# Sliding-window attention trunk on one core: scores by 32 queries and 160 keys, and a written order for the attention stage

## The chip, the cores and the metric

The kernel runs on one core of a Trainium2 chip. The metric is the device time of one execution in microseconds (us). The profile is one execution taken by the hardware profiler; its times are counted from the first instruction. Engines: PE is the matrix engine (PEld its weight loads), DVE the vector engine, ACT the scalar engine, POOL GpSimd, SP the engine that issues most DMAs. L389 is line 389 of the kernel before.

## The reference

One layer of a trunk on 512 tokens of width 2048, all in float32. Conv, state-space and forgetting attention do not occur, since the depth is 1 and mixer 0 is the sliding-window attention:

```python
hn = rmsnorm(x, norm_g)
q, k, v, gate = split(hn @ w_in)              # 32 heads of 64, 4 key/value heads of 64
scores = einsum('qd,jd->qj', q, k) * 64**-0.5 + bias[query - key]   # per head
scores = where(0 <= query - key < 128, scores, min)
m = maximum(scores.max(), sink)
e = exp(scores - m)
probs = e / (e.sum() + exp(sink - m))
y = ((probs @ v) * silu(gate)) @ w_out
x = x + y
g = sigmoid(rmsnorm(x, ple_norm) @ ple_gate)
x = x + (p @ ple_proj) * g
return rmsnorm(x, final_g)
```

## The kernel before

Every product is done in three matmuls of a narrower float32 form: each operand is split into a high part (a cast) and a low part (the rest), and `mm3` (L120 to L122) adds high by high, low by high and high by low. So each weight tile of 128 by 1024 costs one cast on ACT (`whi`, L106; later `bhi`, L575) and one subtraction on DVE (`wlo`, L107; `blo`, L576).

The stages, in order of the program:

1. First steps (L185 to L256): 16 chunks of the model width. Each loads a piece of x and of the first weights, splits both, and PE adds it into the sums of keys (`ktps`), values (`vps`) and the first two query pairs (`qps`). For chunk 0 the weights come in two DMAs, and their first 256 columns are split by DVE alone (L200, L201). `xl` (L202) is the low part of x.
2. Seam (L271 to L305): the sums leave PSUM. Queries go to `q` as high and low halves (`evac_q`), keys are scaled by `rb` (1/rms of every token) and split (`make_key`), values likewise (`split`).
3. Attention and projections, about 84 to 457 us. An outer loop runs over 64 blocks plus 3: block i has d = i // 8, which names four heads (two pairs), and g = i % 8, which names 64 queries. In one pass of the loop PE gets, in this order: two transposes of the probabilities of block i-2 (`turn`, L431), two or three matmuls by the values for block i-3 (`weigh`, L467 and L469), two matmuls of scores for block i (`scores`, L389; one for each pair of heads), and then 7 of the 464 chunk steps of the query and gate projections that are left after the first (`projections`, a step is three matmuls of 512 columns). There are 30 projections, 14 of query pairs and 16 of gates, with 16 steps and two weight tiles each.
4. Output projection, then the gated embedding, both as seven-product block schemes (`ORDER_OUT`, `ORDER_PLE`), and at last four blocks with the norm and the stores. `split_last` (L578 to L586) splits the eight weight tiles of the last product ahead of time, at the places that the table `early` (L954) names: a key (5, 0, 3) means product 5, half 0, after its quarter 3.

In a block of stage 3 the work after the scores is: DVE adds the bias to the high part and then the low part (L398), which also multiplies by `sclq`, the query's 1/rms over 8; a maximum folds the two window ends (L413); a reduction gives the row maximum (L415); ACT takes two exponentials with their sums (L418); DVE a reciprocal (L419); ACT scales the probabilities (L421). After PE's transposes ACT casts to `r` (L433), DVE takes the rest (L434), POOL cuts out the own part (L443, from g = 2 on) and ACT copies half of it (L450); `weigh` reads `r` and `own`. Every second block ACT copies half of the sums to `tmp` (L476) and DVE adds them into `u` (L477). A finished gate projection costs DVE, ACT and DVE one operation each (`open_gate`, L499 to L501), and later one on DVE (`gate_value`, L491).

What sets the order: PE and SP follow the written order throughout (`manual_schedule`). In stage 3 POOL does too; DVE and ACT are ordered by a scheduler that runs when the kernel is built. In the seam and in the last part of stage 4 DVE and ACT are in written order as well. Weight tile n is asked for at the place in the program where it is split (`_make`, L101); the splits are made two tiles ahead of their use (`ahead=2`), with three buffers each for raw, high and low tiles. Since SP waits only for free buffers, it may run ahead of the other engines. Between two passes of the loop, `sum_weights` puts weight additions by DMA on SP and POOL.

The key and value sums, in stage 3, share PSUM with the scores (one buffer of two banks, tag `w`), the transposes (`t`, two), the value sums (`o`, two) and the projections (`p`, two): the sum of projection m takes the bank of m-2.

Of the kernel before, what the change touches and what calls it, by code (L numbers as in the profile page):

```python
# [19 lines left out]
S = 512  # L20
P = 128
# [9 lines left out]
UNITS = S // HB  # L31
BUCKETS = 32
# [7 lines left out]
PAD = 32  # L40
# [13 lines left out]
def trunk_kernel(ctx: ExitStack, tc: tile.TileContext, a: dict):  # L54
# [32 lines left out]
    class Weights:  # L87
# [4 lines left out]

        def add(self, src):
            self.srcs.append(src)
# [6 lines left out]
        def _make(self, i):  # L101
            self.load(i + 1)
# [22 lines left out]
    sinkb = const.tile([P, PAIRS], F32, name="sinkb")  # L125
# [17 lines left out]
    sclq = const.tile([P, UNITS], F32, name="sclq")  # L143
# [24 lines left out]
    q_at = {int(0.5 + 3.516 * (c // 2)) - 2 + c % 2: c for c in range(2, PAIRS)}  # L168
# [15 lines left out]

    for k in range(KC):  # L185
        both = start_pool.tile([P, 2, 768], F32R, tag="w0s", name=f"w0s{k}")
# [50 lines left out]
        if k == 9:  # L237
            run(rsqrt_mean(rstd1, ssq1, D, "r1"))
            for e in range(2):
                for b in range(2):  # L240
                    nc.vector.tensor_scalar_mul(
                        sclq[HB * e : HB * e + HB].rearrange("p (n b) -> p n b", b=2)[:, :, b],
                        rstd1[HB * b : HB * b + HB], HD ** -0.5,
                    )

            rdram = tc.dram_tile([NB, P], F32, name="rdram")
            nc.gpsimd.dma_start(rdram.rearrange("t p -> p t"), rstd1)
            nc.gpsimd.dma_start(rb, rdram.rearrange("t p -> (t p)").partition_broadcast(P))
        if k == 10:
            for e in range(2):  # L250
                nc.sync.dma_start(sinkb[HB * e : HB * e + HB], a["sinks"][e].partition_broadcast(HB))
# [6 lines left out]
    def evac_q(c, ps):  # L258

        q = Q[c] = kvq.tile([P, UNITS, 2, HB], F32R, tag="q", name=f"q{c}", bufs=4)  # L260
        halves = slice(0, 64), slice(64, 128)
        for e in range(2):
            src = ps[halves[e]].rearrange("p (g q) -> p g q", q=HB)
            hi, lo = q[halves[e], :, e], q[halves[1 - e], :, e]
            nc.scalar.copy(hi, src)
            nc.vector.tensor_sub(lo, src, hi.bitcast(F32))


    seam = ExitStack()
    seam.enter_context(  # L270
        tc.manual_schedule(engines={getattr(mybir.EngineType, v) for v in ("PE", "SP", "DVE", "Activation")})  # L271
    )
    for c in range(2):
        evac_q(c, q_ps[c])
# [4 lines left out]
    def make_key(h):  # L279
# [4 lines left out]
        for o in (slice(0, 64), slice(64, 128)):  # L284
            nc.scalar.copy(k[o, 0], kt[t][same])
        for o in (slice(0, 64), slice(64, 128)):
            nc.vector.tensor_sub(k[o, 1], kt[t][same], k[same, 0].bitcast(F32))
# [4 lines left out]
    def split(dst, v):  # L292
        nc.scalar.copy(dst[:, :, 0, :], heads(v))
        nc.vector.tensor_sub(dst[:, :, 1, :], heads(v), dst[:, :, 0, :].bitcast(F32))

    nc.vector.tensor_mul(kt[0], kt_ps[0], rb)
    make_key(0)
# [8 lines left out]
    split(V[0], values[0])  # L306
    seam.close()
# [29 lines left out]
    DV = apool.tile([P, NB - 1, 2, KVH * 2 * HD], F32R, name="DV")  # L337
    diffs = {}

    def make_diff(n):  # L340
# [8 lines left out]
        split(dst.rearrange("p (h l d) -> p h l d", h=KVH, l=2), v)  # L349
# [7 lines left out]
    def first_chores(i):  # L357
        if i == 0:
            for n in range(1, NB):
                make_diff(n)  # L360
        if 1 <= i < NB:
            split(V[i], values[i])
            spread_diff(i)

    def load_bias(d):
        biases[d] = apool.tile([P, 2, P + HB], F32, tag="bias", name=f"bias{d}", bufs=2)
        for e in range(2):
            src = bass.AP(
                tensor=tdram.tensor, offset=tdram.offset + (4 * d + e) * TOEP + HB,
                ap=[[1, HB], [2 * TOEP, 2], [1, P + HB]],  # L370
            )
            nc.sync.dma_start(biases[d][HB * e : HB * e + HB], src)

    def scores(i):

        d, g = divmod(i, UNITS)
        odd = g % 2
# [4 lines left out]
        first = max(g - 2, 0) * HB  # L384
        n = P if g < 2 else P + HB
        s_ps = spsum.tile([P, 2, S], F32, tag="w", name=f"s{i}")
        for u in range(2):
            st = Q[2 * d + u][:, g].rearrange("p e q -> p (e q)")
            nc.tensor.matmul(s_ps[:, u, : 2 * n], st, key[:, :, first : first + n], start=True, stop=True)  # L389
        t = apool.tile([P, 2, 4 + P + HB], F32, tag="t", name=f"t{i}", bufs=4)  # L390
        seen = t[:, :, 65:194] if odd else t[:, :, 0:129]
        pr = t[:, :, 65:193] if odd else t[:, :, 1:129]
        sink = 193 if odd else 0
        nc.gpsimd.tensor_copy(t[:, :, sink], sinkb[:, 2 * d : 2 * d + 2])
        bias = biases[d][:, :, ::-1]

        def add(out, in0, in1):
            nc.vector.scalar_tensor_tensor(  # L398
                out=out, in0=in0, scalar=sclq[:, g : g + 1], in1=in1, op0=ALU.mult, op1=ALU.add
            )  # L400

        if g < 2:
            if g == 0:
                nc.gpsimd.memset(t[:, :, 65:129], MASKED)
            n = HB * (g + 1)
            out = pr[:, :, :n]
            add(out, s_ps[:, :, :n], bias[:, :, 192 - n :])
# [753 lines left out]
```

## Time and profile before

| what | value |
|---|---|
| time, median of 3 runs | 804.19 us (804.07 to 805.76) |
| time of the profiled execution | 804.26 us |
| its span, first to last instruction | 802.4 us |
| mean granted PE clock | 0.996 |
| HBM over the span | 255 GB/s |
| DVE in stage 3 (324 to 445 us), busy | 92.68 of 121 us |
| ACT there | 78.36 of 121 us |
| PE there | 121.00 of 121 us |

A row of a timeline gives the start, the duration, the engine, the line, the operation, what it writes and reads, the size, and in brackets how long the engine had been idle and what ended that. `x2` means that two instructions were merged. Matmuls are pipelined: their shown durations overlap, so a busy PE is not yet a PE at its best pace, and the distance between two starts is what a matmul costs. Groups of instructions give the count, the total busy time and the mean in ns.

### The profile page before, as it was taken

The page shows a single profiled execution, that of the slowest core. Times are in us where ns is not written, and L with a number is a line of the kernel's source. Part 1 is how long each engine was busy: PE and PEld are TensorE (multiplying, and loading weights), DVE is VectorE, ACT ScalarE, POOL GpSimd, SP SyncE. Part 2 cuts the span into 40 slices and gives each one's busy share as a digit, 9 for nine tenths or more (in the row PEclk, how much of TensorE's full clock was granted, in tenths as well). Part 3 has the DMA queues.
Part 4 walks back from the last instruction along what each step waited for, and adds up shares of the span by engine and source line. Part 5 has one row for each costly group of instructions (what it writes and reads, how often), then busy time and mean ns, then how long its engine had stood idle before and what let it go on. Part 6 is the DMA issues. An engine that isn't in the chain of part 4 may idle for free. (4 is left out here: it accounts for less than half of the span.)

```text
span 802.4 us, 10946 instructions
## 1 busy us (share of the span) xinstructions
PE 791.1 (99%) x3763; PEld 660.0 (82%) x3763; DVE 592.1 (74%) x970; ACT 500.5 (62%) x1041; POOL 110.1 (14%) x218
## 2 busy tenths in 40 slices
PE   9999999999999999999999999999999999999995
PEld 7888888888888888888888888888888888888785
DVE  4536886887777776777778897766646756989896
ACT  5624667676667666676666654655668656656855
POOL 0002213122122212112122200030000020200000
PEclk9999999999999999999999999999999999999998
DMA  8863678778687977868685369898513996785532
GB/s 318 327 172 101 183 241 215 228 202 233 172 220 215 218 215 199 221 177 246 159 219 132 105 233 348 333 275 248 195 46 92 372 216 197 156 229 182 182 107 105
DMA packets 45239, 165.15 MB, mean 206 GB/s; under 512 B 5936, under 2 KB 8112, under 8 KB 41344
## 3 DMA queue, kind: packets, MB, share of 16 engines
q1 hardware_dynamic: 38352, 130.59, 47.9%
q0 software_dynamic: 6832, 33.88, 22.4%
q8 instruction: 29, 0.48, 0.2%
q14 instruction: 26, 0.21, 0.1%
HBM read 158.63 MB, written 46.19 MB: 255 GB/s over the span
## 5 line engine op out<-in xcount | busy, mean ns | idle before, releaser
L576 DVE TENSOR_TENSOR blo<-braw,bhi 128x1024 fp32r<-128x1024 f32 x80 | 97.5, 1222 | 39.7 <-ACT bhi L575 39.4
L575 ACT CAST bhi<-braw 128x1024 fp32r<-128x1024 f32 x80 | 84.0, 1051 | 65.8 <-PE g L122 18.9
L122 PE MATMUL gps<-xh,wlo 128*128 128x512 f32 x256 | 100.1, 391 | 0.0
L121 PE MATMUL gps<-xl,whi 128*128 128x512 f32 x256 | 100.1, 391 | 0.0
L120 PE MATMUL gps<-xh,whi 128*128 128x512 f32 x256 | 99.8, 390 | 0.0
L107 DVE TENSOR_TENSOR wlo<-wraw,whi 128x1024 fp32r<-128x1024 f32 x60 | 73.3, 1221 | 20.8 <-ACT whi L106 19.7
L122 PE MATMUL qps<-xh,wlo 128*128 128x512 f32 x224 | 87.8, 392 | 0.0
L120 PE MATMUL o<-bhi,fho 128*128 128x512 f32 x224 | 87.7, 391 | 0.0
L121 PE MATMUL qps<-xl,whi 128*128 128x512 f32 x224 | 87.7, 391 | 0.0
L121 PE MATMUL o<-blo,fho 128*128 128x512 f32 x224 | 87.3, 390 | 0.0
L122 PE MATMUL o<-bhi,flo 128*128 128x512 f32 x224 | 87.2, 389 | 0.0
L120 PE MATMUL qps<-xh,whi 128*128 128x512 f32 x224 | 87.2, 389 | 0.0
L106 ACT CAST whi<-wraw 128x1024 fp32r<-128x1024 f32 x60 | 62.9, 1048 | 26.9 <-PE gps L121 10.6
L418 ACT ACTIVATE t<-t,sm 128x129 f32<-128x129 f32 x128 | 50.6, 397 | 45.9 <-DVE sm L415 45.6
L121 PE MATMUL g<-blo,fhg 128*128 128x512 f32 x192 | 75.0, 391 | 0.7 <-DVE blo L576 0.7
L120 PE MATMUL g<-bhi,fhg 128*128 128x512 f32 x192 | 75.1, 391 | 0.0
L122 PE MATMUL g<-bhi,flg 128*128 128x512 f32 x192 | 74.8, 390 | 0.0
L443 POOL TENSOR_SCALAR_AFFINE_SELECT own<-r 64x512 fp32r<-64x512 f32 (+1 forms) x48 | 34.1, 711 | 291.7 <-DVE r L434 286.2
L122 PEld LDWEIGHTS gps<-xh,wlo 128*128 128x128 f32 x256 | 48.0, 188 | 10.3
L576 DVE TENSOR_TENSOR blo<-grown,bhi 128x1024 fp32r<-128x1024 f32 x32 | 39.1, 1223 | 23.6 <-ACT bhi L575 21.9
L120 PEld LDWEIGHTS gps<-xh,whi 128*128 128x128 f32 x256 | 48.1, 188 | 8.9
L121 PEld LDWEIGHTS gps<-xl,whi 128*128 128x128 f32 x256 | 48.1, 188 | 8.9
(200 smaller groups left out, 1698.0 us busy)
## 6 DMA issues: line engine op xcount, KB each, us to landing
wraw<-in_w_gate_in SPq DMA_DIRECT2D x32, 512.0 KB, 5.6
wraw<-in_w_q SPq DMA_DIRECT2D x28, 512.0 KB, 4.5
w_out<-in_w_out POOLq DMA_DIRECT2D x24, 512.0 KB, 7.4
braw<-in_w_out SPq DMA_DIRECT2D x24, 512.0 KB, 4.3
braw<-in_ple_gate SPq DMA_DIRECT2D x24, 512.0 KB, 4.3
w_out<-in_w_out SPq DMA_DIRECT2D x16, 512.0 KB, 6.7
ple_gate<-in_ple_gate SPq DMA_DIRECT2D x16, 512.0 KB, 5.5
ple_gate<-in_ple_gate POOLq DMA_DIRECT2D x16, 512.0 KB, 7.2
```

Of the source, the lines that this page charges most:

```text
L106: nc.scalar.copy(hi, raw)
L107: nc.vector.tensor_sub(lo, raw, hi.bitcast(F32))
L120: nc.tensor.matmul(ps, sh, mh, start=first, stop=False, skip_group_check=more)
L121: nc.tensor.matmul(ps, sh, ml, start=False, stop=False, skip_group_check=more)
L122: nc.tensor.matmul(ps, sl, mh, start=False, stop=last, skip_group_check=more)
L418: nc.scalar.activation(su, su, AF.Exp, bias=sm[:, u : u + 1], accum_out=sm[:, 2 + u : 3 + u])
L443: nc.gpsimd.affine_select(out=flat(own), in_=flat(r).bitcast(F32), pattern=[[0, 8], [sign, HB]], compare_op=ALU.is_ge, fill=0.0, base=-HB ...
L575: nc.scalar.copy(hi, raw)
L576: nc.vector.tensor_sub(lo, raw, hi.bitcast(F32))
```

## The change

Scores: the two scores matmuls of a block are no longer 64 queries by two heads each, but 32 queries by all four heads (`QB` = 32). A group of 32 queries sees at most 160 keys (`KEYS`) where it was 192, so a scores matmul has 2 x 160 columns where it had 2 x 192; the first four groups of a pair have 64, 128, 192 and 256 columns where they had 256. The adds, the maximum and the bias tile shrink alike, the bias comes in four DMAs of 32 partitions where it was two of 64, the sinks too; `t` has three buffers where it had four, and the scaled probabilities go to a tile of their own (`pr`). POOL fills masked columns in three of the first groups where it was one instruction of 128 columns.

Query scale: `sclq` and its four small instructions go, and the adds become plain additions; instead DVE multiplies each query sum by `rb` in PSUM before it is split (one more instruction of 128x512 for each of the 16 query projections).

Order: DVE and ACT follow the written order from the seam to the end of stage 3, and in the first two chunks of stage 1. In a pass of the loop the parts stand where generators yield; the evacuation of a projection and the splits of keys, values and gates are lists of chores (`chores`, `idle`), one taken after chunk steps 0, 2 and 4. A weight split that falls due is put on `W.todo` and made after chunk step 0 of the next pass. Its raw tile is asked for one tile earlier in the program. Query projections come one place earlier (`q_at`).

End: four places of `early` move later. The pad of `const` grows, and a small pad tile is new. The rest of stages 1 and 4 stays.

```diff
-PAD = 32
+PAD = 48
...
         def _make(self, i):
-            self.load(i + 1)
+            self.load(min(i + 2, len(self.srcs)))
...
         def get(self, i):
-            while len(self.made) <= min(i + self.ahead, len(self.srcs) - 1):
-                self._make(len(self.made))
+            while self.asked <= min(i + self.ahead, len(self.srcs) - 1):
+                self.todo.append(partial_of(self._make, self.asked))
+                self.asked += 1
+            while self.todo and not (self.apart and i < len(self.made)):
+                self.todo.pop(0)()
             return self.made[i]
...
-    q_at = {int(0.5 + 3.516 * (c // 2)) - 2 + c % 2: c for c in range(2, PAIRS)}
+    q_at = {int(0.5 + 3.516 * (c // 2)) - 3 + c % 2: c for c in range(2, PAIRS)}
...
     for k in range(KC):
+        if k == 0:
+            front.enter_context(
+                tc.manual_schedule(engines={getattr(mybir.EngineType, v) for v in ("PE", "SP", "DVE", "Activation")})
+            )
+        if k == 2:
+            front.close()
...
-            for e in range(2):
-                nc.sync.dma_start(sinkb[HB * e : HB * e + HB], a["sinks"][e].partition_broadcast(HB))
+            for h in range(4):
+                nc.sync.dma_start(sinkb[QB * h : QB * h + QB], a["sinks"][h].partition_broadcast(QB))
...
     def evac_q(c, ps):
...
+        def scaled():
+            nc.vector.scalar_tensor_tensor(out=ps, in0=ps, scalar=HD ** -0.5, in1=rb, op0=ALU.mult, op1=ALU.mult)
+
+        def split(low):
+            for e in range(2):
...
+                if low:
+                    nc.vector.tensor_sub(lo, src, hi.bitcast(F32))
+                else:
+                    nc.scalar.copy(hi, src)
+
+        return scaled, partial_of(split, False), partial_of(split, True)
...
+    first_q = [evac_q(c, q_ps[c]) for c in range(2)]
+    for part in (first_q[0][0], first_q[1][0], *first_q[0][1:], *first_q[1][1:]):
+        part()
...
     def scores(i):
...
-        first = max(g - 2, 0) * HB
-        n = P if g < 2 else P + HB
+        number = [min(2 * g + u + 1, 5) * QB for u in range(2)]
         for u in range(2):
-            st = Q[2 * d + u][:, g].rearrange("p e q -> p (e q)")
+            first, n = max(2 * g + u - 4, 0) * QB, number[u]
+            st = Q[d][:, 2 * g + u].rearrange("p h q -> p (h q)")
             nc.tensor.matmul(s_ps[:, u, : 2 * n], st, key[:, :, first : first + n], start=True, stop=True)
...
-            add(t[:, :, 1:193], s_ps[:, :, :n], bias)
-            add(t[:, :, 1:193], s_ps[:, :, n : 2 * n], t[:, :, 1:193])
+            x = t[:, :, 1 : 1 + KEYS]
+            nc.vector.tensor_add(x, s_ps[:, :, :KEYS], bias.unsqueeze(1).to_broadcast([P, 2, KEYS]))
+            nc.vector.tensor_add(x, s_ps[:, :, KEYS : 2 * KEYS], x)
...
     for i in range(blocks + 3):
...
+        before, softmax = softmax, scores(i) if i < blocks else iter(())
+        turned = turn(i - 2) if 2 <= i < blocks + 2 else iter(())
+        value = weigh(i - 3) if 3 <= i else iter(())
+        next(turned, None)        # PE transposes, ACT and DVE r
+        next(value, None)         # PE weigh
+        next(softmax, None)       # PE scores, POOL sink
+        next(turned, None)        # POOL own
+        next(before, None)        # ACT scales block i-1
+        next(softmax, None)       # DVE adds, maximum, reduction
+        first_chores(i, 0)
...
+        for n in range(max(todo, 6)):
+            if n < todo:
+                next(proj)
+            if n == 0:
+                first_chores(i, 1)
+                some(W.todo)
+                some(chores or idle)
+            elif n == 2:
+                next(value, None)     # ACT tmp, DVE u
+                if len(chores) > 1:
+                    some(chores)
+            elif n == 3:
+                next(turned, None)    # ACT own
+                next(softmax, None)   # ACT exponentials
+            elif n == 4:
+                first_chores(i, 2)
+                some(chores or idle)
+            elif n == 5:
+                next(softmax, None)   # DVE reciprocal
...
-    early = {(5, 0, 3): 0, (5, 1, 2): 1, (5, 1, 3): 2, (3, 0, 1): 3, (3, 0, 3): 4, (3, 1, 0): 5, (3, 1, 2): 6}
+    early = {(5, 0, 3): 0, (5, 1, 2): 1, (5, 1, 3): 2, (3, 0, 3): 3, (3, 1, 0): 4, (3, 1, 1): 5, (3, 1, 3): 6}
```

The comments in the loop are added here.

More of the change, by code (lines that the diff above doesn't have):

```diff
@@ L305, in trunk_kernel @@
         )
-    split(V[0], values[0])
-    seam.close()
+    for part in split(V[0], values[0]):
+        part()
     misc = quarter("misc")
@@ L391, in scores @@
[L391 to L400, printed above, removed]
[L402 to L413 removed]
+        W = KEYS + 2
@@ new lines, in scores, with two @@
+        t = apool.tile([P, 2, W], F32, tag="t", name=f"t{i}", bufs=3)
+        at = t[:, 0, 0:1]
+        def two(of, stride, n):
+            return bass.AP(tensor=at.tensor, offset=at.offset + of, ap=[at.ap[0], [stride, 2], [1, n]])
+        late = QB if g >= 2 else 0
+        seen = [t[:, 0, 0 : P + 1], t[:, 1, 1 + late : P + 2 + late] if late else t[:, 1, 0 : P + 1]]
+        both = two(0, W + 1 + late if late else W, P + 1)
+        pr = [t[:, u, 1 + late * u : 1 + late * u + P] for u in range(2)]
@@ L741, in trunk_kernel @@
         pass
-    while due:
-        gate_value()
+    while chores or idle:
+        some(chores or idle)
     during.close()
```

204 lines of the change are left out of this document (112 added, 92 removed).

## The prediction

> **What bounds the kernel now.** I read the page first, then the waits of PE, then PE's timeline for the distance between two starts.
>
> ```profile
> span 802.4 us, 10946 instructions
> PE 791.1 (99%) x3763; PEld 660.0 (82%) x3763; DVE 592.1 (74%) x970; ACT 500.5 (62%) x1041; POOL 110.1 (14%) x218
> ```
>
> ```profile
> PE g L121 <- DVE blo L576: 0.7, 1, 0.7
> ```
>
> PE is busy for all but 11.3 us of the span, and the one wait of any size after the start, as the list of waits has it, is 0.7 us near the end. The shown durations of matmuls overlap, so the pace has to be read from starts. One pass of the attention loop:
>
> ```profile
> 302.88 0.40 PE L122 MATMUL gps<-xh,wlo 128*128 128x512 f32 x1
> 303.11 0.38 PE L431 MATMUL pt<-ident,t 128*128 128x128 f32 x2
> 303.25 0.48 PE L467 MATMUL o<-r,V 128*128 128x256 f32 x2
> 303.57 0.28 PE L469 MATMUL o<-own,DV 128*128 128x256 f32 x1
> 303.69 0.51 PE L389 MATMUL s<-k,q 128*128 128x384 f32 x2
> 304.04 0.39 PE L120 MATMUL gps<-xh,whi 128*128 128x512 f32 x1
> ```
>
> From start to start: 0.23 us for 512 columns (302.88 to 303.11), 0.12 for 256 (303.57 to 303.69), and two of 384 take 0.35 (303.69 to 304.04), 0.175 each. Two transposes of 128 and two of 256 together take 0.46 (303.11 to 303.57), so with 0.12 for each of the latter a transpose costs 0.11. PE goes from one kind to the next without a gap: the kernel runs at the pace at which PE takes matmuls, and only columns removed from PE, or gaps between its starts, move the end. A pass is 7 steps x 3 x 0.227 + 0.93 = 5.7 us.
>
> **The change part by part.**
>
> *Scores on PE.*
>
> ```profile
> L389 PE MATMUL s<-k,q 128*128 128x384 f32 x96 | 24.7, 338 | 0.0
> L389 PE MATMUL s<-k,q 128*128 128x256 f32 x32 | 6.4, 282 | 0.0
> ```
>
> The 96 matmuls of 384 columns become 96 of 320. No row has 320; its bounds are the 256 row (0.12) and the 384 row (0.175), and I take the middle, 0.147: 96 x 0.028 = 2.7 us gained (bounds 0 and 5.3; the steps 128, 256, 384, 512 lie near a line above 256, so I hold the middle to within 0.01, 1 us in all). Of the 32 others, 8 stay at 256; 24 get 64, 128 or 192 columns. No row has such a scores matmul; the nearest are the transpose (0.11) and the 256 row, so I take 0.11: 24 x 0.01 = 0.2 gained. The widest bound is the 512 row, 0.23: 24 x 0.11 = 2.6 lost. Sum: 2.9 gained.
>
> [...]
>
> *The wait near the end.*
>
> ```profile
> 744.05 1.05 ACT L583 CAST last<-grown 128x1024 fp32r<-128x1024 f32 x1
> 745.13 1.23 DVE L584 TENSOR_TENSOR low<-grown,last 128x1024 fp32r<-128x1024 f32 x1 [0.26 <-ACT last L583]
> 746.27 1.22 DVE L576 TENSOR_TENSOR blo<-braw,bhi 128x1024 fp32r<-128x1024 f32 x1
> 750.66 1.22 DVE L576 TENSOR_TENSOR blo<-braw,bhi 128x1024 fp32r<-128x1024 f32 x1
> 753.54 2.35 DVE L576 TENSOR_TENSOR blo<-braw,bhi 128x1024 fp32r<-128x1024 f32 x2
> ```
>
> ```profile
> 750.87 0.39 PE L120 MATMUL g<-bhi,fhg 128*128 128x512 f32 x1
> 751.93 0.50 PE L121 MATMUL g<-blo,fhg 128*128 128x512 f32 x1 [0.68 <-DVE blo L576]
> 752.27 0.40 PE L122 MATMUL g<-bhi,flg 128*128 128x512 f32 x1
> 754.81 0.50 PE L121 MATMUL g<-blo,fhg 128*128 128x512 f32 x1
> 755.15 0.40 PE L122 MATMUL g<-bhi,flg 128*128 128x512 f32 x1
> ```
>
> PE loses 1.06 - 0.23 = 0.83, then 0.11 and 0.11 (steps of 0.34): 1.05 us, more than the waits list tells. In the new table `early` the split at 744.05 and 745.13 comes two quarters later, so the pair behind it moves up by 1.14 (745.13 to 746.27), and DVE's chain up to 750.66 with it: that tile is then done at 750.7, and PE asks for it at 750.87 + 0.23 = 751.1. The next (753.54) has again one split ahead of it, comes 1.14 earlier too and is done at 753.6; PE, no longer late, asks at 750.87 + 13 x 0.227 = 753.8. Later quarters come 2.7 us apart, with one split of 1.2 moved between each. Gain 1.05; if the second margin of 0.2 fails, a few tenths less.
>
> *Late `r` and `own`.* The list of waits does not show these either:
>
> ```profile
> 218.05 0.48 PE L467 MATMUL o<-r,V 128*128 128x256 f32 x2
> 218.47 0.38 PE L469 MATMUL o<-own,DV 128*128 128x256 f32 x1
> 218.69 0.40 PE L389 MATMUL s<-k,q 128*128 128x256 f32 x2
> ```
>
> ```profile
> 400.35 0.39 PE L469 MATMUL o<-own,DV 128*128 128x256 f32 x1
> 400.57 0.39 PE L389 MATMUL s<-k,q 128*128 128x256 f32 x2
> ```
>
> At 218, 0.42 and 0.22 stand where the pass above has 0.32 and 0.12: 0.2 lost. It happens three times (the first, and the end of the last, are shown). The scheduler had put the subtraction of `r` behind other DVE work; in the written order it is DVE's first work of a pass. Gain 0.6 (0 if something else is then late by as much).
>
> *DVE in written order.*
>
> ```profile
> 84.00:204.00 120.00, 120.00 (x584) 100.58 (x583) 94.32 (x190) 81.64 (x220) 23.94 (x50) 1.00 0.80 224
> L398 DVE SCALAR_TENSOR_TENSOR t<-s,sclq,t 128x384 f32<-128x384 f32 x48 | 29.6, 617 | 1.2
> L434 DVE TENSOR_TENSOR r<-pt,r 128x256 fp32r<-128x256 f32 x64 | 26.8, 419 | 19.4 <-ACT r L433 18.6
> L501 DVE SCALAR_TENSOR_TENSOR gate<-gps,gate 128x512 f32<-128x512 f32 x16 | 10.9, 680 | 0.0
> ```
>
> The first row is a stretch of the stage: PE 120.00 of 120, DVE 94.32, ACT 81.64. Each big add goes from 617 to about 419 + 64 x 1.02 = 485 ns (plain add of 320, between the 256 and 512 rows): 96 x 0.13 = 12.7 gained on DVE. The scaling of queries adds 16 x 0.68 = 10.9. So DVE keeps its load, 79% of the stage, and has no gain to hand on. It hides as long as nothing that PE needs stands too late in the order. The deadline that comes nearest is `own`: ACT copies it in the same pass in which it casts `r`, and PE reads it in the next.
>
> ```profile
> L106 ACT CAST whi<-wraw 128x1024 fp32r<-128x1024 f32 x60 | 62.9, 1048 | 26.9 <-PE gps L121 10.6 <-PE qps L121 10.0 <-DMA wraw<-in_w_gate_in 5.9
> L433 ACT CAST r<-pt 128x256 fp32r<-128x256 f32 x64 | 23.0, 360 | 3.1 <-PE pt L431 2.6
> L421 ACT ACTIVATE t<-t,sm 128x128 f32<-128x128 f32 x128 | 44.6, 396 | 10.2 <-DVE sm L419 9.2
> L476 ACT COPY tmp<-o 64x256 f32<-64x256 f32 x64 | 23.5, 368 | 12.7 <-DVE u L477 11.7
> L450 ACT CAST own<-own 64x256 fp32r<-64x256 f32 x48 | 19.4, 405 | 23.4 <-POOL own L443 22.5
> L285 ACT CAST k<-kt 64x512 fp32r<-64x512 f32 x8 | 5.0, 619 | 1.6 <-DVE kt L296 1.5
> ```
>
> In the heaviest pass of the written order ACT has before it: `r` 0.36, two scalings 0.79, a weight cast 1.05, two key casts 1.24, two `tmp` 0.74, then `own` 0.41: 4.6 us, begun some 0.4 after the pass (end of the transposes). So `own` is there at 5.0; PE asks at 5.7 + 0.46 = 6.1. The margin is 1.1 us. I take no new gap, and bound it by the rival below.
>
> *Weights.* A split is now made one pass after it is asked for, two tiles ahead of its use. A tile is 8 steps, 5.4 us and more; of two tiles ahead at most a pass (5.7) and cast and subtraction (2.3) go, and 3 us stay. That raw tiles stand earlier in SP's order changes nothing while SP runs ahead and waits for buffers only: cost nothing.
>
> *The first steps.*
>
> ```profile
> 9.37 0.93 ACT L206 CAST w0s<-w 128x256 fp32r<-128x256 f32 x2 [0.24 <-DMA w<-in_w_first]
> 9.82 0.50 PE L215 MATMUL qps<-xh,w0s 128*128 128x512 f32 x1
> ```
>
> The new order puts L201 ahead of L202, so PE's second pair of matmuls comes sooner; but chunk 1 waits for its weights' DMA (ACT idle until 9.37, PE at 9.82), so the time is only spent waiting there: nothing. At the seam PE's first projection waits for query bank 0, now scaled first:
>
> ```profile
> 69.14 0.58 ACT L265 CAST q<-qps 64x512 fp32r<-64x512 f32 x1 [4.47 <-PE qps L122]
> 72.39 0.40 PE L120 MATMUL gps<-xh,whi 128*128 128x512 f32 x1
> ```
>
> From 69.14: two scalings 0.68 each on DVE, then two low halves at 0.7 (near L501's size): 2.8, so 71.9, and PE is there at 72.39. Nothing, margin 0.5.
>
> The sum: 2.9 + 1.05 + 0.6 = 4.55. The profiled execution took 804.26 us (span 802.4), 0.07 above the median of the three runs: **799.7 us**.
>
> **The rivals.**
>
> *The written order makes `own` late.* If DVE's reciprocal of the pass before, on which ACT's scalings wait, comes more than 1.1 us after PE's transposes, everything behind it on ACT (weight cast, `tmp`, `own`, exponentials) is late, and PE waits at L469. For it: DVE's heaviest pass, with 1.22 of weights, 0.84 of `u` and 1.4 of a key or query split, is about as long as a pass, 5.7. Against: every second pass has no `u`, and the stage stands at 79%. With 0.2 us on average over the 48 passes that have an `own`, 9.6 us are lost: 804.3 - 4.6 + 9.6 = 809 us, slower.
>
> [...]
>
> *A smaller stall of that kind*, 0.1 us per pass: 4.8 lost, 804.5, no change.
>
> *Narrow matmuls are dear.* If the 24 of 64 to 192 columns cost what 512 do, 2.6 + 0.2 go: 802.5. For it: no row shows them. Against: 128-column transposes take 0.11.
>
> *The change doesn't do what it says* in the weights part (SP already ran ahead); this is in the sum as nothing. Were the end's gain only moved to the next tile, the time would be 800.7.
>
> **How the numbers follow.** A measurement of this kernel can tell 0.2%, 1.6 us, from no change. No new gap, 64% (its own range 798.7 to 801.2: 1 us for the middle of the 320 columns, 0.6 + 1.05 that may not come); dear narrow matmuls 10%; the small stall 10%; `own` late 16%. Faster: 64 + 10, 0.74; same 0.10; slower 0.16. The range 798.7 to 804.2 leaves out the slow rival and a part of the small stall.
>
> **What would show it.** The 320-column scores matmuls start 0.147 apart; the step from L120 to L121 where PE waited near the end is 0.23; no 0.42 from L467 to L469; PE 100% in the stretches of the attention stage, the stage some 3.5 us shorter. I am wrong if PE's waits name `own`, `r`, `pr` or `wlo`, or if ACT waits for the reciprocal well after PE's transposes.

## The result, and the profile after

The kernel after the change took 798.83 us (median of 6 runs, 797.95 to 799.88), the kernel before beside it 804.56 us (6 runs, 803.75 to 805.76): a ratio of 0.9927, 95% interval 0.9915 to 0.9938, 5.7 to 5.9 us faster. The direction was as predicted; the gain was 1.2 to 1.3 us larger than the sum of 4.55, so that 0.9927 of 804.19, 798.3, lies under the lower end of the range, 798.7. Three terms of the sum came about as forecast; the gain that it lacked is in matmuls that it took as unmoved.

From the page of the kernel after, the span and the busy times:

```profile
span 796.6 us, 10995 instructions
PE 786.3 (99%) x3763; PEld 658.3 (83%) x3763; DVE 588.9 (74%) x1014; ACT 499.1 (63%) x1041; POOL 113.1 (14%) x234
```

The whole of PE's list of waits, and a stretch of the attention stage (columns as before: PE, PEld, DVE, ACT, POOL busy, clock, DMA share, GB/s):

```profile
PE warm_ps L142 <- PEq L1234: 0.8, 1, 0.8
```

```profile
84.00:204.00 120.00, 120.00 (x590) 100.78 (x589) 92.91 (x205) 81.35 (x222) 24.54 (x52) 1.00 0.76 208
```

The wait near the end has gone from the list. PE still sets the time, and DVE and ACT carry about what they did: 92.91 and 81.35 us of 120, against 94.32 and 81.64. One pass of the loop, PE's timeline:

```profile
204.61 0.39 PE L129 MATMUL gps<-xh,wlo 128*128 128x512 f32 x1
204.84 0.38 PE L477 MATMUL pt<-ident,pr 128*128 128x128 f32 x2
204.97 0.48 PE L519 MATMUL o<-r,V 128*128 128x256 f32 x2
205.29 0.28 PE L521 MATMUL o<-own,DV 128*128 128x256 f32 x1
205.41 0.46 PE L424 MATMUL s<-k,q 128*128 128x320 f32 x2
205.71 0.39 PE L127 MATMUL gps<-xh,whi 128*128 128x512 f32 x1
```

Two scores matmuls of 320 columns take 0.30 (205.41 to 205.71), 0.150 each; everything else in this group of narrow matmuls is as before, to 0.01. The groups by shape that answer to the terms of the sum:

```profile
L424 PE MATMUL s<-k,q 128*128 128x320 f32 x96 | 22.3, 313 | 0.0
L424 PE MATMUL s<-k,q 128*128 128x64 f32 x8 | 1.6, 195 | 0.0
L449 DVE TENSOR_TENSOR t<-s,bias 128x320 f32<-128x320 f32 x48 | 23.1, 481 | 0.0
L450 DVE TENSOR_TENSOR t<-s,t 128x320 f32<-128x320 f32 x48 | 23.6, 492 | 1.7
```

The plain adds take 481 and 492 ns, where 485 was estimated. Both programs have 3763 matmuls, and kind by kind (projection, transpose, weighing, scores and so on) they stand in the same order, so PE's starts can be compared one by one, and the distance from each start to the next added up by kind. That gives where the time came from (us, negative is gained; before and after are one execution each):

| stretch of PE's work | predicted | measured |
|---|---|---|
| up to the first scores | 0 | -0.36 |
| attention stage: scores | -2.9 | -3.02 |
| attention stage: weighing (`r`, `own`) | -0.6 | -0.49 |
| attention stage: projections between | 0 | -1.03 |
| attention stage: transposes | 0 | -0.03 |
| output and gated embedding, first part | 0 | -0.15 |
| near the end (table `early`) | -1.05 | -1.17 |
| after PE's last matmul | 0 | +0.46 |
| span, with rounding | -4.55 | -5.78 |

A distance between starts can charge a matmul's cost to the one behind it, and in the passes with g = 0 it does. There the scores are now 64 and 128 columns where they were twice 256. PE in such a pass, before and after:

```profile
127.74 0.40 PE L389 MATMUL s<-k,q 128*128 128x256 f32 x2
127.98 0.40 PE L120 MATMUL gps<-xh,whi 128*128 128x512 f32 x1
128.21 0.40 PE L121 MATMUL gps<-xl,whi 128*128 128x512 f32 x1
```

```profile
127.01 0.33 PE L424 MATMUL s<-k,q 128*128 128x64 f32 x2
127.18 0.45 PE L127 MATMUL qps<-xh,whi 128*128 128x512 f32 x1
127.47 0.40 PE L128 MATMUL qps<-xl,whi 128*128 128x512 f32 x1
```

The two scores take 0.17 instead of 0.24, but the first projection matmul behind them steps by 0.29 instead of 0.23. Over the eight such passes the scores gain 0.52 and the first matmuls behind them lose 0.43. So of the 3.02 some 2.6 are a gain, and the other projection matmuls gained more than the 1.03 shown: 1.33 in the 48 passes with g of 2 and more.

### The profile page after: what moved, and what is told of

Read it like the earlier page. It is cut to its first block, busy times and chain, and to the rows that moved or that the text cites. A ratio compares the mean times of both kernels' runs of the same rounds, so it can differ in the third digit from the quotient of the medians.

```text
span 796.6 us, 10995 instructions
## 1 busy us (share of the span) xinstructions
PE 786.3 (99%) x3763; PEld 658.3 (83%) x3763; DVE 588.9 (74%) x1014; ACT 499.1 (63%) x1041; POOL 113.1 (14%) x234
## 5 line engine op out<-in xcount | busy, mean ns | idle before, releaser
L482 ACT CAST r<-pt 128x256 fp32r<-128x256 f32 x64 | 23.8, 371 | 71.8 <-PE pt L477 71.4
L493 POOL TENSOR_SCALAR_AFFINE_SELECT own<-r 64x512 fp32r<-64x512 f32 (+1 forms) x48 | 32.4, 675 | 254.9 <-DVE r L483 254.9
L483 DVE TENSOR_TENSOR r<-pt,r 128x256 fp32r<-128x256 f32 x64 | 27.1, 424 | 55.7 <-ACT r L482 55.0
```

The costliest lines, as they stand in the source:

```text
L482: nc.scalar.copy(rh, src)
L483: nc.vector.tensor_sub(rl, src, rh.bitcast(F32))
L493: nc.gpsimd.affine_select(out=flat(own), in_=flat(r).bitcast(F32), pattern=[[0, 8], [sign, HB]], compare_op=ALU.is_ge, fill=0.0, base=-HB ...
```

## The experiments

All rest on the kernel after the change unless said otherwise. An interval of a ratio is about 1 us to either side, so terms below that are read from PE's starts. How far one execution can be trusted there is shown by the repetition first.

**The same kernel again (e5_again).** No edit but a blank line.

> The kernel after the change, unchanged, once more, on the chip and in the company of the runs below. It says what of the accounting is of the kernel and what is of one execution. Of the kernel by the traces so far: the attention stage 370.0 us from the first scores to the first output matmul, within 0.1. Of one execution: the first steps (the same first chunks began their steady pace at 12.44 us in the trace of after, 12.40, 12.37 and 12.86 in three kernels with the same first chunks, 12.82 in before), so anything from 12.3 to 12.9; and the wait for the last splits (0 in after; 0.64, 0.20 and 0.50 in the three experiments that have the new table, 1.31 with the old one), so anything from 0 to 0.7. Ratio to before 0.9927 again, 0.992 to 0.994.

Measured: 0.9932 (0.9919 to 0.9944). The attention stage took 369.93 us against 369.95: repeatable to a few hundredths. The first steps reached their steady pace at 11.89 us, earlier than expected; over the thirteen executions of after and its variants it lay between 11.89 and 12.87, over before and e10, its variant, at 12.82 and 12.94. So of the 0.36 there nothing is told from what executions vary by. The stretch after PE's last matmul was 9.9 us here, 9.5 to 10.3 over after and its variants, and 9.3 in before and e10: some tenths are given back there; why was not tried.

**Scores over 192 keys again (e1_wide).** 80 of the 128 scores matmuls; 32 columns of each copy are computed and not read.

```diff
             first, n = max(2 * g + u - 4, 0) * QB, number[u]
+            if g >= 3:
+                first, n = first - QB, n + QB
...
+            a0, b0 = (QB, KEYS + 2 * QB) if g >= 3 else (0, KEYS)
-            nc.vector.tensor_add(x, s_ps[:, :, :KEYS], ...)
+            nc.vector.tensor_add(x, s_ps[:, :, a0 : a0 + KEYS], ...)
```

> The kernel after the change with the scores matmuls of the passes g = 3 to 7 taken over 192 keys again (384 columns; the 32 first of each copy are computed and not read), 80 of the 128 scores matmuls; every other engine does what it did, the output is the same. Steps measured so far: 384 columns 0.175 us in the trace of before, 320 columns 0.150 us in the trace of after. Both theories: +80 x 0.025 = +2.0 us in the scores' own steps. The theories differ in the projections: their matmuls of 512 columns took 0.038 us a pass more than 0.2267 each before the change and 0.015 after it, 1.0 us over the stage. Theory 'width' (the wide scores are what slows the matmuls behind them): 5/8 of that 1.0 comes back, 0.65, so about +2.65 us in all. Theory 'order' (what the other engines do at that time slows them): the projections stay as in after, +2.0 us in all. Margins around r and own should not move; PE's last matmul goes later by the same sum. Rival to both: the scores' width was hidden behind something and nothing changes, 0.

Measured: 0.9945 (0.9933 to 0.9958). The scores' steps grew by 2.04, as expected; the timeline shows 0.36 for two where after has 0.30:

```profile
206.29 0.51 PE L426 MATMUL s<-k,q 128*128 128x384 f32 x2
206.65 0.40 PE L127 MATMUL gps<-xh,whi 128*128 128x512 f32 x1
```

The projections did not slow down (-0.17). So, in after's layout, the columns carry the scores' term and nothing else: theory "width" is out for the 1.03. Near the end this execution lost 0.64 that after did not (see e3 and e11).

**VectorE and ScalarE left to the scheduler (e2_scheduler).**

```diff
-    during.enter_context(tc.manual_schedule(engines={... ("PE", "SP", "DVE", "Activation", "Pool")}))
+    seam.enter_context(tc.manual_schedule(engines={... ("PE", "SP", "DVE", "Activation")}))
...
     for part in split(V[0], values[0]):
         part()
+    seam.close()
...
+    during.enter_context(tc.manual_schedule(engines={... ("PE", "SP", "Pool")}))
     load_bias(0)
```

> The kernel after the change with the work of VectorE and ScalarE in the attention stage left to the scheduler again (the written order is kept for TensorE, SyncE and GpSimd there, and for VectorE and ScalarE in the seam up to the first split of the values); the instructions are the same ones. Theory 'width' (scores' columns are what was gained): the late r and own come back at most, +0.5 us, and the projections' pace stays as in after. Theory 'order' (the written order makes the projections' matmuls of 512 columns come at 0.2274 instead of 0.2286 us): +0.5 + 1.0 = +1.5 us. Rival: with the parts cut up as they now are, the scheduler puts softmax behind chores, own comes after TensorE asks for it in the passes whose margin is below 0.5 us, and stalls of several tenths in many of the 64 passes add up to 5 us or more.

Measured: 0.9930 (0.9918 to 0.9943). The stage took 0.65 longer: one stall at its start costs 0.8, and the weighing takes 0.15 less than in after, because a late `own` that after has once (see e4) does not come here. PE's list of waits names the stall:

```profile
PE s L423 <- DVE t L445: 0.6, 1, 0.6
```

So neither theory "order" (+1.5) nor the rival (5 and more) holds: with the parts cut as they now are, the scheduler finds an order as good as the written one but for one place, and for `own` a better one: its copy ends at least 1.16 us before PE takes it, in all 48 passes. The late `r` and `own` of before are not the mark of a scheduler as such; and the order is out, too, as the cause of the 1.03.

**The old table `early` (e3_old_table).**

```diff
-    early = {..., (3, 0, 3): 3, (3, 1, 0): 4, (3, 1, 1): 5, (3, 1, 3): 6}
+    early = {..., (3, 0, 1): 3, (3, 0, 3): 4, (3, 1, 0): 5, (3, 1, 2): 6}
```

> The kernel after the change with the table of the last eight splits as it was before. The prediction took 1.05 us for the new table (a wait of TensorE near the end, for the split's low half on VectorE), the traces show 1.17 us between the output matmuls and the last one. Theory 'the table does it': the wait of TensorE comes back near 751 us less the 5 us gained earlier, about +1.1 us, and nothing else moves. Rival 'something else did it, such as the raw pieces landing sooner': 0, and no wait in the list.

Measured: 0.9927 (0.9913 to 0.9940), which cannot be told from after in time; the trace can. PE's timeline, and DVE's just before:

```profile
745.72 0.39 PE L127 MATMUL g<-bhi,fhg 128*128 128x512 f32 x1
747.05 0.50 PE L128 MATMUL g<-blo,fhg 128*128 128x512 f32 x1 [0.94 <-DVE blo L637]
747.39 0.40 PE L129 MATMUL g<-bhi,flg 128*128 128x512 f32 x1
```

```profile
740.25 1.23 DVE L645 TENSOR_TENSOR low<-grown,last 128x1024 fp32r<-128x1024 f32 x1 [0.27 <-ACT last L644]
741.39 1.22 DVE L637 TENSOR_TENSOR blo<-braw,bhi 128x1024 fp32r<-128x1024 f32 x1
745.78 1.22 DVE L637 TENSOR_TENSOR blo<-braw,bhi 128x1024 fp32r<-128x1024 f32 x1
```

The wait is back, with its two late steps, 1.31 in all against after. In after DVE begins the same tile at 744.30, not 745.78, and PE goes on at its pace:

```profile
744.30 1.22 DVE L637 TENSOR_TENSOR blo<-braw,bhi 128x1024 fp32r<-128x1024 f32 x1
745.80 0.39 PE L127 MATMUL g<-bhi,fhg 128*128 128x512 f32 x1
746.03 0.39 PE L128 MATMUL g<-blo,fhg 128*128 128x512 f32 x1
746.26 0.39 PE L129 MATMUL g<-bhi,flg 128*128 128x512 f32 x1
```

The prediction read this mechanism rightly. But the margin is narrow: of the runs with the new table, e1, e4, e8, e12 and e13 took 0.4 to 0.8 more than after in this stretch, the others 0.2 or less.

**The third split moved too (e11_table).**

```diff
-    early = {(5, 0, 3): 0, (5, 1, 2): 1, (5, 1, 3): 2, (3, 0, 3): 3, ...}
+    early = {(5, 0, 3): 0, (5, 1, 2): 1, (3, 0, 2): 2, (3, 0, 3): 3, ...}
```

> The kernel after the change with the third of the last eight splits asked for three steps later in the table, at (3, 0, 2) instead of (5, 1, 3). In the traces with the new table the wait for the split's low half (one matmul, near 747 us) was 0 in five of eight and 0.2, 0.4 and 0.5 in three, with some 0.2 more behind it; VectorE reaches that split behind the low half of this entry, 1.14 us a split. Theory 'VectorE is late by what is queued ahead of it': moving the entry behind it takes the wait away in every run, up to 0.7 us and some 0.25 us on a mean, and never a gain over a run without the wait. Rival 'the entry then comes too late itself or pushes the next ones': a wait of 0.3 to 1.2 us at a later matmul, near 750 to 760 us.

Measured: 0.9947 (0.9928 to 0.9966), a miss. PE lost 1.4 near 747 us and 0.6 at an earlier matmul near 714. The entry did not go behind the wanted tile but in front of it, as DVE's timeline shows:

```profile
745.35 1.22 DVE L645 TENSOR_TENSOR low<-grown,last 128x1024 fp32r<-128x1024 f32 x1
746.48 1.22 DVE L637 TENSOR_TENSOR blo<-braw,bhi 128x1024 fp32r<-128x1024 f32 x1
```

I had mistaken which entry stands where; the run still gives the price again: one split ahead of the wanted tile, 1.14, is 1.2 us of wait.

**`own` issued two steps later (e4_own_later).**

```diff
             elif n == 3:
-                next(turned, None)
                 next(softmax, None)
...
             elif n == 5:
                 next(softmax, None)
+                next(turned, None)
```

> The kernel after the change with the copy of own across partitions (ScalarE) issued two steps later in each pass, behind the pass's two exponentials, which take 1.0 us in the trace (0.41 + 0.19 + 0.39 + 0.19, overlapping); nothing else moves but the exponentials, 0.4 us earlier. The prediction had own 1.1 us ahead of TensorE in the fullest pass and all others looser: then 1.0 us later costs nothing, 0 to 0.3 us. The trace of after shows margins of 0.05, 0.16, 0.36, 0.42, 0.47, 0.6 and 0.89 three times, a median of 2.07 of 48: then the nine passes below 1.0 stall by 4.3 us together, 2.8 to 8 us with other chores between, and TensorE waits for the copy at own's matmul. Rival: a stall in one pass gives the next ones slack, so that only the first of neighbouring passes pays, 1 to 2 us.

Measured: 0.9994 (0.9986 to 1.0003); the weighing took 5.53 us more, which is nearly the whole gain of the change. ACT's and PE's rows of one of the passes, and PE's list of waits:

```profile
178.33 0.18 ACT L457 ACTIVATION_READ_ACCUMULATOR t<-t,sm 128x1 f32 x1
178.36 0.48 PE L519 MATMUL o<-r,V 128*128 128x256 f32 x2
178.54 0.40 ACT L503 CAST own<-own 64x256 fp32r<-64x256 f32 x1
178.99 0.38 PE L521 MATMUL o<-own,DV 128*128 128x256 f32 x1
```

```profile
PE o L521 <- ACT own L503: 3.0, 7, 0.8
```

PE starts 0.05 after the copy's end (178.54 + 0.40) in nine passes of the 48, the number of those whose distance in after was below 1.0. The list of waits shows 3.0 of the 5.5; the rest is again only in the distances of starts.

The prediction's margin of 1.1 in the heaviest pass was too large. In after, eight passes have `own` 0.16 to 0.89 before PE takes it, and one has no margin at all:

```profile
125.70 0.60 ACT L563 ACTIVATE gps<-gate 128x512 f32<-128x512 f32 x1 [2.19 <-DVE gate L562]
126.33 0.41 ACT L503 CAST own<-own 64x256 fp32r<-64x256 f32 x1
126.42 0.48 PE L519 MATMUL o<-r,V 128*128 128x256 f32 x2
126.78 0.39 PE L521 MATMUL o<-own,DV 128*128 128x256 f32 x1
```

PE takes `own` 0.05 after its copy, the distance at which it starts when it is held up in e4. The two `r` matmuls take 0.36 (126.42 to 126.78) where others take 0.32, and `own` steps by 0.23 (to 127.01, above) where others step by 0.12: 0.15 us lost, in e5 again 0.14, and no list of waits names it. Ahead of `own` on ACT stands a gate's activation that waited 2.19 us for DVE; the prediction had added up ACT's work before `own`, without such a wait.

**Weights asked for one split ahead, as before (e8_asked_late).**

```diff
-            self.load(min(i + 2, len(self.srcs)))
+            self.load(min(i + 1, len(self.srcs)))
```

> The kernel after the change with the raw weights asked for one split ahead, as before the change, not two. The prediction costed this at nothing. Theory 'nothing': the attention stage stays at 370.0 us within 0.1, no wait of TensorE for a split. Rival 'with parts of the splits popped once in each pass, the DMA of 512 KB now ends too late for the split in its pass': waits of VectorE and ScalarE for wraw, and TensorE's for the split behind them, 0.3 us or more in some passes, 2 to 5 us in all.

Measured: 802.6 us in one execution beside 804.86 (median of before), the stage 3.4 us longer, two stalls. The first, on ACT and PE:

```profile
109.09 1.05 ACT L110 CAST whi<-wraw 128x1024 fp32r<-128x1024 f32 x1 [3.73 <-DMA wraw<-in_w_gate_in]
110.16 0.74 ACT L530 COPY tmp<-o 64x256 f32<-64x256 f32 x2
110.81 0.40 ACT L503 CAST own<-own 64x256 fp32r<-64x256 f32 x1
111.26 0.39 PE L521 MATMUL o<-own,DV 128*128 128x256 f32 x1 [1.83 <-ACT own L503]
```

In DMA issues on SP's queue, that raw tile is asked for at 102.53 here and at 93.21 in after (first row here, second row after), and lands about 6.5 us after it is asked.

```profile
102.53 0.42 SPq L103 DMA_DIRECT2D wraw<-in_w_gate_in  x1
93.21 0.58 SPq L103 DMA_DIRECT2D wraw<-in_w_gate_in  x1
```

In these rows ACT keeps to the written order: the cast that waited 3.73 us holds back `tmp` and `own` behind it (at 110.16 and 110.81, where after has them at 106.85 and 107.50), and it is `own` that PE stands for, not the weight. The rival was right in its kind: the written order loses 3.4 us without the earlier request. What the earlier request would do in the kernel before was not tried.

**The first two chunks left to the scheduler (e7_front_sched).**

```diff
-                tc.manual_schedule(engines={... ("PE", "SP", "DVE", "Activation")})
+                tc.manual_schedule(engines={... ("PE", "SP")})
```

> The kernel after the change with VectorE and ScalarE left to the scheduler in the first two chunks. The prediction costed the written order there at nothing, because chunk 1 waits for its own weights' DMA. Theory 'the landing decides': steady pace from 12.3 to 12.9 us, as in all runs so far, whatever the order; TensorE waits 0.4 us in the first pair of chunk 0 again. Theory 'the order is worth the 0.36 us seen between the two first traces': 12.7 us or later.

Measured: 798.6 us in one execution; steady pace at 12.44, the first scores at 82.93, both as in after. The written order of the first chunks is worth nothing, as predicted.

**Where the probabilities lie (e6, e9, e10, e12, e13).** Left were the 1.03 in the projections. In before the first nine matmuls of 512 columns behind the narrow ones take 0.224 to 0.236 each and then 0.2267, the same sequence in nearly every pass to a nanosecond; in after, with g of 2 and more, only the first three are slow. The table gives the ns by which the twelve matmuls behind the narrow ones exceed 12 x 0.2267, by the kind of pass, from the second such pass on. Where there are three values, they take turns from one pass of that g to the next, as the three tiles of `pr` do (the probabilities that the transposes load).

```
                         g=2        g=3        g=4        g=5        g=6        g=7
before                    42         43         43         43         42         43
after                     14         14         14         14         14         14
e1_wide                   14         10         10         10         10         10
e6_odd_pr            0/47/32   47/47/47   47/47/47    0/47/32    0/47/32    0/47/32
e9_wide_pr           32/0/22   47/47/16   47/47/16    32/0/22    32/0/22    32/0/22
e12_behind                32         47         47         32         32         32
e13_both                  22         16         16         22         22         22
e10_before_even           41         41         41         42         41          0
```

e6 begins the probabilities on an odd element, as before had them:

```diff
-        T[i] = apool.tile([P, 2, P], F32, tag="pr", ...)
+        T[i] = apool.tile([P, 2, P + 4], F32, tag="pr", ...)[:, :, 1 : 1 + P]
```

> The kernel after the change with the tile of the scaled probabilities, which the transposes load as their stationary operand, made 132 wide and read from its second element, as the probabilities lay inside the softmax tile before the change; same instructions, same output. The question is the 1.0 us by which the projections' matmuls came faster behind the narrow ones, which neither the scores' width nor the order of VectorE and ScalarE brought back (0.010 and 0.014 us a pass over the steady pace in those runs, 0.042 before the change). Theory 'alignment of the transposes' stationary operand': the excess goes back to 0.04 us in the 48 passes with g of 2 and more, +1.3 us. Rival 'other addresses or other steps of the narrow ones': 0, the excess stays at 0.014.

Measured: 0.9936 (0.9921 to 0.9951); the projections +0.98, where the theory had 1.3; but in a third of the passes with g of 2, 5, 6 and 7 nothing is lost. Its control e9 has the same wide tile, read from the first element (`[:, :, :P]`):

> The control of e6_odd_pr: the kernel after the change with the tile of the scaled probabilities 132 wide too, so that what lies behind it in SBUF moves by the same 96 bytes, but read from its first element. In e6_odd_pr the projections took 0.98 us more than in after and the pace behind the narrow matmuls was slow again. Theory 'odd start': projections as in after, within 0.1 us, 3 slow matmuls in the passes with g of 2 and more. Rival 'the move of what lies behind it (r, own, u)': +0.98 us as in e6_odd_pr.

Measured: the projections +0.55 with an even start, so the first theory falls, and so does the rival's +0.98: it is neither. Three passes on end of e9, first and thirteenth start of the projections behind the narrow matmuls (2.74, 2.72 and 2.75 us for the same twelve matmuls):

```profile
200.07 0.39 PE L127 MATMUL gps<-xh,whi 128*128 128x512 f32 x1
...
202.81 0.39 PE L127 MATMUL gps<-xh,whi 128*128 128x512 f32 x1
...
205.73 0.39 PE L127 MATMUL gps<-xh,whi 128*128 128x512 f32 x1
...
208.45 0.39 PE L127 MATMUL gps<-xh,whi 128*128 128x512 f32 x1
...
211.36 0.39 PE L127 MATMUL qps<-xh,whi 128*128 128x512 f32 x1
...
214.11 0.39 PE L127 MATMUL qps<-xh,whi 128*128 128x512 f32 x1
```

e10 goes the other way, in the kernel before: its softmax tile is 200 wide and begun three elements in, so the probabilities start on an even one.

```diff
-        t = apool.tile([P, 2, 4 + P + HB], F32, tag="t", name=f"t{i}", bufs=4)
+        t = apool.tile([P, 2, 8 + P + HB], F32, tag="t", name=f"t{i}", bufs=4)[:, :, 3:]
```

> The kernel before the change with its softmax tile 200 wide instead of 196 and begun three elements in, so that the probabilities that the transposes load start at element 4 or 68 and no longer at 1 or 65; same instructions. Theory 'odd start' (what the change gained in the projections it gained by copying the probabilities into a tile of their own): the projections of the attention stage take 1.0 us less than in before, 0.7 to 1.3, 803.5 us where before has 804.5; the scores and the weighing stay. Rival 'something else that the change moved': 0.

Measured: 0.9992 (0.9979 to 1.0005); the projections -0.59, not the -1.0 of the theory, and mostly from the passes with g = 7, which lose nothing at all now, while those with g of 2 to 6 stay. An even or odd start alone does not explain that.

e12 moves what lies behind `pr` by 96 bytes (as in e9) and leaves `pr` in place; e13 puts 64 bytes ahead of `pr` and 32 behind it:

```diff
# e12
+        if i == 0:
+            apool.tile([P, 24], F32, name="pad3")
         r = apool.tile([P, 2, 256], F32R, tag="r", ...)
# e13
+        if i == 0:
+            apool.tile([P, 16], F32, name="pad3")
         T[i] = apool.tile([P, 2, P], F32, tag="pr", ...)
...
+        if i == 0:
+            apool.tile([P, 8], F32, name="pad4")
         r = apool.tile([P, 2, 256], F32R, tag="r", ...)
```

> The kernel after the change with 96 unused bytes of SBUF put between the tiles of the scaled probabilities (pr) and the tiles allocated after them (r, own, u): pr stays where it is in after, at 202240 + 1024 n, the others move by 96 bytes as in e9_wide_pr. In e9_wide_pr the three pr tiles lay 1056 bytes apart, and the time that the twelve matmuls behind the narrow ones lose to a steady 0.2267 depended, to a nanosecond, on which of the three a pass's transposes load: 32, 0 and 22 ns with g of 2, 5, 6 and 7 (47, 47 and 16 with g of 3 and 4) for pr at +0, +32 and +64 bytes from a multiple of 1024 away from the first; in after it is 14 in every pass with g of 2 and more. Theory 'addresses of both': every pass now shows the first of these, 32 (g 2, 5, 6, 7) and 47 (g 3, 4): 32 x 0.032 + 16 x 0.047 = 1.8 us in place of 48 x 0.014 = 0.7, so +1.1 us in the stage. Theory 'pr alone': 14 in every pass as in after, 0. Theory 'the pattern is of the rotation and not of the place': the three values still take turns, +0.55.

> The kernel after the change with 64 unused bytes ahead of the pr tiles and 32 behind them: the pr tiles lie at 202304 + 1024 n, the tiles after them where e9_wide_pr has them. Theory 'addresses of both': every pass shows what e9_wide_pr's passes with pr at +64 showed, 22 ns with g of 2, 5, 6 and 7 and 16 with g of 3 and 4: 32 x 0.022 + 16 x 0.016 = 1.0 us in place of 0.7, +0.3 us in the stage, and 0.8 us less than e12_behind, though the same instructions run and the same tiles follow. Theory 'pr does not count, only what follows it': the same as e12_behind, whatever that is.

Measured, one execution each: e12's passes show 32 and 47, e13's 22 and 16, as the theory "addresses of both" had it. The projections cost +1.20 in e12 and +0.39 in e13, near its +1.1 and +0.3. For the stage the theory missed: in e12 the scores' own steps came 0.42 sooner, in e13 transposes and weighing 0.29 later, so that the stage is 0.70 longer than after's in e12 and 0.65 in e13, not 0.8 apart. What the place takes from one kind of matmul it partly gives to another; over the stage, e6, e9, e12 and e13 lie 0.76, 0.56, 0.70 and 0.65 above after. (e12's 803.45 us holds two waits for first weights ahead of the stage besides, 1.9 us in the list; e13 took 799.67.)

## Where the prediction failed, and what it had right

- **The step that failed: projections taken as unmoved.** A pass was counted as 7 steps x 3 x 0.227 plus the narrow matmuls, with the same 0.227 before and after; the sum has no term for the pace of the 512-column matmuls, the range no room for it, and no reason was given. Behind the narrow ones they came 1.03 us faster over the stage (1.33 in the passes with g of 2 and more), which is most of the 1.2 missing; the first steps (0.36) and the end (0.46 back) nearly cancel. e1 and e2 rule out the scores' width and the other engines' order. e9, e12 and e13 show that the same instructions lose 0 to 47 ns a pass there by where `pr` and the tiles behind it lie in SBUF, a span that holds before's 42 and after's 14. Whether the move of the tiles, all of it or some, is what took before to after is not shown: the layouts of `q`, `t` and `pr` all changed, only `pr` and what lies behind it were moved one at a time, and that moved the stage by at most 0.76. What in PE makes the place matter is open too.
- **PE as the bound; the scores' columns.** Right. 320 columns step by 0.150 where the middle of the rows gave 0.147, so the 96 big ones gave 2.4 instead of 2.7, and e1 takes 2.04 back. The 24 narrow ones gave 0.6 by their own starts (64 columns 0.031, 192 columns 0.090), but 0.43 of it is paid by the first matmuls behind them, so about 0.2 is left, as forecast. The 0.11 for a transpose, from which that forecast came, was a misreading: the two transposes step by 0.109 and 0.026, and the first `r` matmul by 0.20, so the price of a narrow matmul was right by luck. The rival "narrow matmuls are dear" is out: with what is behind them they cost what 256 columns did, not what 512 do.
- **The wait near the end.** Right in mechanism and size (1.05 predicted, 1.17 measured, 1.31 in e3). The rival that the gain is only moved to the next tile did not come: the steps there are 0.23 in after. That a margin of some tenths might fail was said, and in five runs some of it did.
- **Late `r` and `own`.** Right in size (0.6, measured 0.49). The trace of before bears out the chain for the pass at 218: DVE subtracts a weight first, then `r`, and the copy of `own` that hangs on it ends at 218.41, 0.06 before PE's `own` matmul.

```profile
215.57 1.23 DVE L107 TENSOR_TENSOR wlo<-wraw,whi 128x1024 fp32r<-128x1024 f32 x1
216.82 0.42 DVE L434 TENSOR_TENSOR r<-pt,r 128x256 fp32r<-128x256 f32 x1
218.01 0.40 ACT L450 CAST own<-own 64x256 fp32r<-64x256 f32 x1 [2.80 <-POOL own L443]
```

So it was `own`'s matmul that was held up there. That the written order is what cures it is not borne out: e2 has the scheduler and not the stalls.

- **`own`'s margin.** This step failed, at a cost of 0.15 us: 1.1 us was taken for the heaviest pass, while one pass has nothing left and eight have 0.16 to 0.89. No stall of 0.1 or 0.2 us a pass came, but the rival "`own` late" was not far: e4 issues the copy two steps later and loses 5.5 us. That a late operation on ACT holds up those behind it, on which this rival rests, is what e8 shows: `tmp` and `own` stand behind a cast that waited 3.73 us, and PE waited 1.83 us for `own`.
- **Weights asked for earlier, costed at nothing.** No run shows what it gained from before to after, but the reason was wrong: SP does not run ahead so far that the place of the request is free. e8 without it asks 9.3 us later and loses 3.4 us in the stage.

## What to carry to other kernels

Where PE sets the end, count columns by the distances of starts and add up those distances by kind before and after: lists of waits here missed 0.4 of a 1.3 us stall and 2.5 of a 5.5 us one. Take a narrow matmul together with the one behind it, since that one may pay its price: over the eight passes with g = 0, 0.43 of 0.52 us. A written order is only as good as its tightest deadline: list the margins of every pass, with the waits of each engine in them, since a heaviest pass worked out by hand can be off by the whole margin, and keep loads early enough that no engine in written order meets one: in e8 one cast's wait of 3.73 us for its load became 1.83 us of PE's. Differences of 0.1% between two layouts can come from addresses alone (0.56 to 0.76 us over the stage in e6, e9, e12 and e13); a control that only pads tiles, as e9 was, tells them from a mechanism, and the sum over the stage tells what of it reaches the end.

## What the runs showed of the hardware that was not expected

A 512-column matmul does not always step by 0.2267: behind a group of narrow ones, up to nine step by 0.224 to 0.236 at a granted clock of 1.00. How many do goes, to a nanosecond, with the place of `pr` and the tiles behind it: from e12 to e13 `pr` moves by 64 bytes and the rest stays, and passes lose 22 and 16 ns instead of 32 and 47, with no wait in any list there. A matmul of 64 columns steps by 0.031 and one of 192 by 0.090, but one of 128 behind one of 64 by 0.142, and one of 512 behind those two by 0.286: the three together take 0.46, where 256, 256 and 512 took 0.47.
